# A hybrid decoder block on one core: rotary DMAs and the rotary table moved to the load queue, an eviction put first, keys split a step sooner, two multiplications moved in the tail

## The chip, the core and the metric

The kernel runs on one core of one Trainium2 chip. The core has five engines that run side by side, each with its own instruction queue that it works through in order: PE (TensorE, matmuls), ACT (ScalarE), DVE (VectorE), POOL (GpSimd) and SP (SyncE, which here does nothing but start DMAs). They wait for each other through semaphores. DMAs are started from the queues of SP and ACT; an engine that starts a DMA first waits, like for any other instruction, until what the DMA needs is there, and everything behind it on that engine waits with it. The metric is the device time of one execution in microseconds (us), lower is better. "Span" is the profiled part of one execution, from the first instruction to the last.

## The reference

One layer, everything in float32, 1024 positions of width 1024:

```python
h = x + 1/2 * SwiGLU_1(rms(x))                     # hidden width 2816
u = rms(h);  [q | k | v | p | gate_logits] = u @ W_in
A: q, k: rotate the first 16 of 64 dims (rotary);  12 heads in 3 groups with
   (window, dilation) = (128, 1), (512, 4), (2048, 16); softmax attention;
   the groups are merged per head slot by their softmax denominators; @ W_A
B: p: trailing means over 2/4/8/16 positions minus p, per-group linear map, scale; @ W_B
h = h + (sigmoid(gA) * yA + sigmoid(gB) * yB) @ W_o
h = h + 1/2 * SwiGLU_2(rms(h))
out = rms_final(h)
```

The rotation of a head of q or k, for each position with its angle: `out = [x1*c - x2*s, x2*c + x1*s, rest]`, where x1 and x2 are dims 0 to 7 and 8 to 15 and c, s are a table of cosines and sines over positions.

## The kernel before

**Matrix products.** A float32 operand is split in two parts, a high one (`hi`, a rounded copy made by ACT) and a low one (`lo = x - hi`, by DVE or POOL), and a product is the sum of three matmuls (hi·hi, lo·hi, hi·lo). On top of that the wide products use a seven-product scheme of the Strassen kind: sums and differences of quarter matrices are formed by DVE, seven products are taken instead of eight, and the results are combined. A product of the projections is 12 matmuls of 128x512 (`product`, L316).

**Stages in order of time.** FFN 1 up; FFN 1 down (`Down`, L788: seven products, each in steps of 24 matmuls; ACT L746 makes the high parts `bhi_f` of the weights and `ahi_f` of the activations, L750 the low parts `blo_f`, `alo_f` on DVE or, every fourth, on POOL, L732 loads the activations `g_f`, L766 forms sums of weights); the mixer's projection W_in ("mix"); attention and the pooling branch; W_o; FFN 2 up; FFN 2 down and the final norm ("tail").

**Order of the work.** Most of the kernel stands under `tc.manual_schedule()`: each engine executes in the order in which the Python code issues. So the order of calls in the loops is the order of each engine's queue.

**The table.** In FFN 1 down, a dictionary `tasks` (L1346) hangs small jobs on steps: at step 4 the raw table is loaded in rows by position (`load_rope`), at step 10 `make_tables` (L1312) transposes six 128x128 blocks on PE (L1317), ACT copies them out of PSUM (L1318), and eight DMAs on ACT's queue (L1322) store them in DRAM, ordered for reading back.

**The projection loop** (L1387). `items` lists the products in order, one a step; within an operation the order is (1, 6, 2, 7, 5, 4, 3). In step k: the result of product k-1 is taken out of its bank first if it is a product 1 (`out(1)`); then the operand of step k+2 is formed and split (`mix_operand`: DVE L354, L358, L362, L367 for sums, ACT L304 the high part, DVE or POOL L307 the low part); the sigmoid of a finished gate (`activate`, L1081); the twelve matmuls of product k; the result of product k-1 if it wasn't a 1 (`out`: ACT L1057 for 1, DVE L1060 for 6, ACT L1062 for 2, DVE L1064 for 7, L1068 for 5, L1071 for 4, L1074 for 3); and last the pending jobs in `later`, each a generator that is resumed some steps on. Products 5 and 3 use the same PSUM bank (`key` "v"; 1 and 2 share "x"): product 3 starts from zero in it, so it has to wait until `out(5)` has read it. `raw` tiles are the weights, loaded by SP (L67, L69).

**Jobs.** `rotate` (L1097, six of them, for the pairs of q or k): stores the projected rows to DRAM (L1101, two DMAs), some steps later loads the first 16 dims of each head into one tile `ro` (L1107, two DMAs), shuffles (L1111), multiplies with the table's two parts (L1112, L1113), reloads the table for the next group where it is the last user (`load_table`, L1190, DMA L1195 on SP), adds (L1117), and stores the rotated dims back (L1120, two DMAs). All but the table's load are on ACT's queue. `turn` stores v on SP (L1138). `split_late` splits weights that are needed later and stores them on SP (L1215, L1216, L1220). `window` is the pooling branch (L1151 to L1175).

**Attention** (loop at L1839). A step q takes two blocks of scores (L1592 on PE), exponentials (ACT L1619), transposes the exponentials (PE L1639), splits them (`ehi`, ACT L1651; `elo`, DVE L1654), and multiplies with v (L1672). The q and k of the next group lie in a ring: loaded by SP (L1231), split in quarters by `split_ring` (ACT L1238 the high part, POOL L1239 the low part). For the second group of the ring, `uses[1]`, the quarters are split in steps 3 and 4; they are read by the scores from step 4 on.

**Tail.** In FFN 2 down's last two products DVE adds the result (L793) to h by tiles t; with the product before the last `low_half` (L2150) takes the squares of the low half of tile 4+t (ACT L2153), and for tiles 5 and 6 at once multiplies the low half with the final gain (`with_gain`, DVE L2160); with the last product the high halves follow (L2164), then the norm's power (L2168, L2169) and the scaled output (L2174, L2178, L2184).

## Time and profile before

| | |
|---|---|
| median of 3 runs | 1920.37 us (1918.9 to 1920.75) |
| profiled execution | 1922.71 us |
| its span | 1920.9 us |
| mean granted PE clock | 0.996 |
| mean DMA rate | 172 GB/s |

How to read it: rows of a timeline give the start in us, the duration in us, the engine and line, the operation, `output<-input`, the shape, and in brackets how long the engine stood idle before and what released it. Consecutive similar instructions are one row (xN). A `q` behind an engine's name (SPq, ACTq) is its queue of DMA starts. The granted clock is the share of full TensorE clock that the chip allowed.

### The profile page before, as it was taken

The page shows a single profiled execution, that of the slowest core. Times are in us where ns is not written, and L with a number is a line of the kernel's source. Part 1 is how long each engine was busy: PE and PEld are TensorE (multiplying, and loading weights), DVE is VectorE, ACT ScalarE, POOL GpSimd, SP SyncE. Part 2 cuts the span into 40 slices and gives each one's busy share as a digit, 9 for nine tenths or more (in the row PEclk, how much of TensorE's full clock was granted, in tenths as well). Part 3 has the DMA queues.
Part 4 walks back from the last instruction along what each step waited for, and adds up shares of the span by engine and source line. Part 5 has one row for each costly group of instructions (what it writes and reads, how often), then busy time and mean ns, then how long its engine had stood idle before and what let it go on. Part 6 is the DMA issues. An engine that isn't in the chain of part 4 may idle for free.

```text
span 1920.9 us, 24690 instructions
## 1 busy us (share of the span) xinstructions
PE 1894.7 (99%) x8822; PEld 1566.7 (82%) x8822; DVE 1330.4 (69%) x1975; ACT 772.3 (40%) x1394; POOL 711.1 (37%) x532
## 2 busy tenths in 40 slices
PE   9999999999999998999999999999999999999998
PEld 8888888888778887888887888888888888878886
DVE  6886566557677776667886787888665556577777
ACT  7323333334335542334444673263333333333344
POOL 4433333332122353444555265643333333312131
PEclk9999999999999999999999999999999999999999
DMA  4154223336466636575668877643433223453564
GB/s 188 62 200 155 83 95 125 109 129 209 133 206 218 202 97 183 186 261 188 220 236 307 301 232 266 249 176 119 172 115 127 83 90 120 142 197 132 198 213 164
DMA packets 144131, 330.78 MB, mean 172 GB/s; under 512 B 17672, under 2 KB 39176, under 8 KB 142472
## 3 DMA queue, kind: packets, MB, share of 16 engines
q1 hardware_dynamic: 136008, 308.52, 46.6%
q10 hardware_dynamic: 8000, 20.69, 3.1%
q8 instruction: 69, 1.13, 0.2%
q14 instruction: 54, 0.44, 0.1%
HBM read 229.61 MB, written 99.55 MB: 171 GB/s over the span
## 4 chain that ended last, share of the span: by engine, by line
PE 36%; DVE 4%; DMA 3%; issue 3%; ACT 2%; POOL 2%; SPq 0%; ACTq 0%; DVEq 0%; POOLq 0%
PE d_f L788 7%; PE wo L1984 3%; PE yp L1731 1%; PE u_mixm L316 1%; PE u_f20b L316 1%; PE u_f21a L316 1%; PE u_f210a L316 1%; PE u_f29b L316 1%; PE u_f29a L316 1%; PE u_f28b L316 1%; PE u_f27b L316 1%; PE u_f27a L316 1%; PE u_f26b L316 1%; PE u_f26a L316 1%; PE u_f25b L316 1%
## 5 line engine op out<-in xcount | busy, mean ns | idle before, releaser
L788 PE MATMUL d_f<-bhi_f,alo_f 128*128 128x512 f32 x616 | 241.4, 392 | 3.6 <-POOL alo_f L750 3.0
L788 PE MATMUL d_f<-bhi_f,ahi_f 128*128 128x512 f32 x616 | 241.3, 392 | 1.5 <-ACT ahi_f L746 1.0
L788 PE MATMUL d_f<-blo_f,ahi_f 128*128 128x512 f32 x616 | 240.2, 390 | 0.0
L750 POOL TENSOR_TENSOR alo_f<-g_f,ahi_f 128x512 fp32r<-128x512 f32 x60 | 83.8, 1414 | 281.8 <-ACT ahi_f L746 257.5
L316 PE MATMUL u_mixm<-xhi_t_mix,wc_mixm 128*128 128x512 f32 x608 | 158.8, 392 | 4.1 <-ACT wc_mixm L304 4.1
L788 PEld LDWEIGHTS d_f<-bhi_f,alo_f 128*128 128x128 f32 x616 | 116.0, 188 | 30.9 <-POOL alo_f L750 5.5
L788 PEld LDWEIGHTS d_f<-bhi_f,ahi_f 128*128 128x128 f32 x616 | 116.1, 188 | 26.7 <-ACT ahi_f L746 2.3
L316 PEld LDWEIGHTS u_mixm<-xhi_t_mix,wc_mixm 128*128 128x128 f32 x608 | 114.0, 189 | 28.2 <-ACT wc_mixm L304 4.8
L788 PEld LDWEIGHTS d_f<-blo_f,ahi_f 128*128 128x128 f32 x616 | 116.1, 189 | 23.9
L316 PE MATMUL u_mixm<-xhi_b_mix,wc_mixm 128*128 128x512 f32 x456 | 120.9, 393 | 3.4 <-ACT wc_mixm L304 1.5
L307 POOL TENSOR_TENSOR wc_mixm<-s_mixm,wc_mixm 128x512 fp32r<-128x512 f32 x52 | 78.1, 1503 | 107.9 <-ACT wc_mixm L304 103.6
L316 PEld LDWEIGHTS u_mixm<-xhi_b_mix,wc_mixm 128*128 128x128 f32 x456 | 84.5, 188 | 22.7 <-issue 1.6
L304 ACT ACTIVATE wc_mixm<-s_mixm 128x512 fp32r<-128x512 f32 x76 | 47.5, 628 | 119.6 <-DVE s_mixm L358 44.1
L746 ACT ACTIVATE ahi_f<-g_f 128x1024 fp32r<-128x1024 f32 x84 | 81.9, 975 | 4.4 <-DMA g_f<-gs_f 4.3
L316 PE MATMUL u_mixm<-xlo_t_mix,wc_mixm 128*128 128x512 f32 x304 | 82.0, 392 | 0.0
L307 POOL TENSOR_TENSOR wc_mixm<-raw,wc_mixm 128x512 fp32r<-128x512 f32 x40 | 58.4, 1461 | 48.0 <-ACT wc_mixm L304 36.1
L1984 PE MATMUL wo<-w_o,o_hi 128*128 128x512 f32 x224 | 69.4, 391 | 0.2 <-DVE merge L1799 0.2
L746 ACT ACTIVATE bhi_f<-s_f1w 128x512 fp32r<-128x512 f32 x55 | 32.7, 628 | 89.8 <-DVE s_f1w L766 71.5
L746 ACT ACTIVATE bhi_f<-s_f2w 128x512 fp32r<-128x512 f32 x55 | 32.6, 627 | 89.5 <-DVE s_f2w L766 81.8
L316 PEld LDWEIGHTS u_mixm<-xlo_t_mix,wc_mixm 128*128 128x128 f32 x304 | 57.6, 190 | 12.2
L750 DVE TENSOR_TENSOR alo_f<-g_f,ahi_f 128x1024 fp32r<-128x1024 f32 (+1 forms) x48 | 57.5, 1199 | 8.1 <-ACT ahi_f L746 8.1
L316 PE MATMUL u_mixm<-xlo_b_mix,wc_mixm 128*128 128x512 f32 x228 | 61.1, 390 | 0.0
(1332 smaller groups left out, 4756.3 us busy)
## 6 DMA issues: line engine op xcount, KB each, us to landing
g_f<-gs_f SPq DMA_DIRECT2D x70, 512.0 KB
gs_f<-y_f SPq DMA_DIRECT2D x88, 256.0 KB
raw<-in_w2a_dram SPq DMA_DIRECT2D x35, 512.0 KB
raw<-in_w2b_dram SPq DMA_DIRECT2D x35, 512.0 KB
gs_f<-gb_f SPq DMA_DIRECT2D x46, 256.0 KB
raw<-in_w1a_dram SPq DMA_DIRECT2D x22, 512.0 KB
raw<-in_w3a_dram SPq DMA_DIRECT2D x22, 512.0 KB
raw<-in_w1b_dram SPq DMA_DIRECT2D x22, 512.0 KB
```

The costliest lines, as they stand in the source:

```text
L304: ac.activation(w[:, 0], src, AF.Copy)
L307: eng.tensor_tensor(w[:, 1], src, w[:, 0].bitcast(F32), op=OP.subtract)
L316: pe.matmul(p, a, b, start=(start and n == 0), stop=(n == 11), skip_group_check=not start)
L746: ac.activation(hi[:, c], src, AF.Copy)
L750: eng.tensor_tensor(lo[:, d], src[:, o], hi[:, d].bitcast(F32), op=OP.subtract)
L788: pe.matmul(self.banks[m][t], l, r, start=(first and q == 0), stop=(last and q == 2))
L1731: pe.matmul(p, a, b, start=(j == 0), stop=(j == 11))
L1984: pe.matmul(banks[m][t], l, r, start=(st == 0 and j == 0 and q == 0), stop=(st == 1 and j == 1 and q == 2))
```

## The change

1. The rotation's 36 DMAs (L1101, L1107, L1120) go from ACT's queue to SP's. In `rotate` the table's reload moves one step later, behind the add, and the add moves ahead of the step's end.
2. The table is put in another layout. A copy on POOL (`reorder`, at step 9) interleaves the rows so that the transposes give blocks that one SP DMA stores, in place of the eight on ACT. The two multiplications with the table read it in strips of 128.
3. `out(5)` is treated as `out(1)`: it is issued first in its step, ahead of the next operand's instructions; the sigmoid of a gate then follows a step sooner.
4. `split_ring(uses[1], ...)` is issued in steps 2 and 3 instead of 3 and 4.
5. `with_gain(5)` and `with_gain(6)` are issued with tile 7's low half instead of each with its own tile.

PE's instructions and their order are the same as before. SP goes from 731 instructions to 768, ACT from 1334 to 1290.

```diff
--- before.py
+++ after.py
@@ -1013,7 +1013,7 @@
 
 
     qk_dram = [dram.tile([2, 2, HD, S], F32, name=f"qk{u}") for u in range(HPAIRS * GROUPS)]
-    table_dram = dram.tile([16, 2 * GROUPS, 2, 4, P], F32, name="table")
+    table_dram = dram.tile([2 * GROUPS, P, P], F32, name="table")
     v_dram = [dram.tile([P, 2, S], F32, name=f"v{u}") for u in range(HPAIRS * GROUPS)]
     pool_dram = [dram.tile([P, 2, S], F32, name=f"pool{g}") for g in range(4)]
     gate_dram = [dram.tile([P, 2, S], F32, name=f"gate{d}") for d in range(KT)]
@@ -1098,26 +1098,27 @@
             g, y = self.g, self.y
             u = self.hp * GROUPS + g
             for a in (1, 0):
-                nc.scalar.dma_start(qk_dram[u][a].rearrange("h d c -> (h d) c"), y[a])
+                nc.sync.dma_start(qk_dram[u][a].rearrange("h d c -> (h d) c"), y[a])
                 yield 1
             yield 3
             ro = tmp(f"ro{u}").rearrange("p (a c) -> p a c", a=2)
             places = [qk_dram[u][:, :, :16, c].rearrange("a h r c -> (a h) r c") for c in (LOWS, HIGHS)]
             for t in range(2):
-                nc.scalar.dma_start(ro[t * HD:(t + 1) * HD, 0, :], places[t])
+                nc.sync.dma_start(ro[t * HD:(t + 1) * HD, 0, :], places[t])
             yield 3
             tab = tables[g]
 
             ve.stream_shuffle(ro[:, 1, :], ro[:, 0, :], [i ^ 8 for i in range(32)])
-            ve.tensor_tensor(ro[:, 1, :], ro[:, 1, :], tab[:, 1, :], op=OP.mult)
-            ve.tensor_tensor(ro[:, 0, :], ro[:, 0, :], tab[:, 0, :], op=OP.mult)
+            for n in (1, 0):
+                part = ro[:, n, :].rearrange("p (j c) -> p j c", j=4)
+                ve.tensor_tensor(part, part, tab[:, :, n], op=OP.mult)
+            yield 1
+            ve.tensor_tensor(ro[:, 0, :], ro[:, 0, :], ro[:, 1, :], op=OP.add)
             if self.hp == 1 and g + 1 < GROUPS:
                 load_table(g + 1)
             yield 1
-            ve.tensor_tensor(ro[:, 0, :], ro[:, 0, :], ro[:, 1, :], op=OP.add)
-            yield 1
             for t in range(2):
-                nc.scalar.dma_start(places[t], ro[t * HD:(t + 1) * HD, 0, :])
+                nc.sync.dma_start(places[t], ro[t * HD:(t + 1) * HD, 0, :])
 
         def turn(self):
             yield 1
@@ -1188,10 +1189,10 @@
     tables = {}
 
     def load_table(g):
-        tables[g] = keep.tile([P, 2, HALF], F32, tag="gain", bufs=1, name=f"table{g}_in")
+        tables[g] = keep.tile([P, 4, 2, P], F32, tag="gain", bufs=1, name=f"table{g}_in")
         for t in range(2):
-            src = table_dram[:, 2 * g + t].rearrange("c s j p -> c (s j p)")
-            dst = tables[g][t * HD:(t + 1) * HD].rearrange("p s c -> p (s c)")
+            src = table_dram[2 * g + t].rearrange("(c q) p -> c (q p)", c=16)
+            dst = tables[g][t * HD:(t + 1) * HD].rearrange("p j s c -> p (j s c)")
             nc.sync.dma_start(dst, src[None].to_broadcast([4, 16, 1024]))
 
     def split_late(i):
@@ -1309,17 +1310,19 @@
             given.append(own_row("rope")[:, :768])
             nc.sync.dma_start(given[0].rearrange("p (i c) -> p i c", i=GROUPS * NT), c_rope)
 
+        def reorder():
+            given.append(own_row("turn")[:, :768])
+            src, dst = (v.rearrange("p (b x) -> p b x", b=2 * GROUPS) for v in given)
+            gp.tensor_copy(dst.rearrange("p b (c q) -> p b c q", c=16), src.rearrange("p b (q c) -> p b c q", c=16))
+
         def make_tables(tag):
             tab = own_row("table")[:, :768]
             for c, n in ((0, 4), (4, 2)):
                 p = bank(tag, f"table_{c}")
                 for j in range(n):
-                    pe.transpose(p[:, j * P:(j + 1) * P], given[0][:, (c + j) * P:(c + j + 1) * P], ident)
+                    pe.transpose(p[:, j * P:(j + 1) * P], given[1][:, (c + j) * P:(c + j + 1) * P], ident)
                 ac.activation(tab[:, c * P:(c + n) * P], p[:, :n * P], AF.Copy)
-            tab = tab.rearrange("p (b c) -> p b c", c=P)
-            for n in range(8):
-                j, a = divmod(n, 2)
-                nc.scalar.dma_start(table_dram[:, :, a, j], tab[16 * n:16 * n + 16])
+            nc.sync.dma_start(table_dram.rearrange("b m p -> m b p"), tab.rearrange("p (b c) -> p b c", c=P))
 
         def rows_first(t, tag):
             rs = [Rows(X_mix, "b11", h[t][:, LOWS], t, tag), Rows(X_mix, "b21", h[t][:, HIGHS], t, tag)]
@@ -1345,6 +1348,7 @@
 
         tasks = {
             4: [(load_rope,), (load_small,)],
+            9: [(reorder,)],
             10: [(make_tables, "mm")],
             31: [(inverse, 0)],
             32: [(inverse, 1), (scale_in_place, 0)],
@@ -1385,8 +1389,8 @@
         later, results = [], {}
         load_table(0)
         for k in range(len(items) + 4):
-            if k - 1 in results and items[k - 1][1] == 1:
-                mixes[items[k - 1][0]].out(1, results.pop(k - 1))
+            if k - 1 in results and items[k - 1][1] in (1, 5):
+                mixes[items[k - 1][0]].out(items[k - 1][1], results.pop(k - 1))
             mix_operand(k + 2)
             if k + 3 < len(items) and items[k + 3][1] in (7, 4):
                 mix_operand(k + 3, 2)
@@ -1862,9 +1866,9 @@
             if i > 1 and 0 < u < len(uses) - 1:
                 split_ring(uses[u + 1], i - 2)
                 split_ring(uses[u + 1], i)
-            if q in (3, 4):
-                split_ring(uses[1], q - 3)
-                split_ring(uses[1], q - 1)
+            if q in (2, 3):
+                split_ring(uses[1], q - 2)
+                split_ring(uses[1], q)
             end_branches()
             exponents(2 * q)
             exponents(2 * q + 1)
@@ -2152,8 +2156,9 @@
         y, st = h_tile(f"n4_{t}"), small.tile([P, 4], F32, tag="nlast", name=f"nst_last{t}")
         ac.activation(y[:, LOWS], h[t][:, LOWS], AF.Square, scale=D ** -0.5, accum_out=st[:, 0:1])
         ends[t] = y, st
-        if t in (5, 6):
-            with_gain(t)
+        if t == 7:
+            with_gain(5)
+            with_gain(6)
 
     def with_gain(t):
         y = ends[t][0]
```

## The prediction

> **What bounds the kernel now.** I read the busy shares first, then the list of waits of TensorE (PE), then the timelines of the engines around each wait.
>
> ```profile
> span 1920.9 us, 24690 instructions
> PE 1894.7 (99%) x8822; PEld 1566.7 (82%) x8822; DVE 1330.4 (69%) x1975; ACT 772.3 (40%) x1394; POOL 711.1 (37%) x532
> ```
>
> PE is busy for 1894.7 of 1920.9 us: only 26.2 us are idle. The change leaves PE's instructions and their order alone, so it can win only idle time or time at a low clock. The waits of PE (engine, tile, line, what it waited for: us in total, times, longest) say which idle time is in reach:
>
> ```profile
> PE u_mixm L316 <- ACT wc_mixm L304: 5.7, 3, 4.1
> PE d_f L788 <- POOL alo_f L750: 3.0, 6, 0.7
> PE s L1592 <- POOL xhi_b_mix L1239: 1.3, 1, 1.3
> PE u_mixm L316 <- ACT y_m L1057: 0.7, 2, 0.4
> ```
>
> There is a second loss. Cut into windows (length, five busy times, granted clock, DMA share, GB/s), three stretches of 20 us have a low clock:
>
> ```profile
> 500.00:520.00 20.00, 18.64 (x73) 14.33 (x72) 12.54 (x18) 6.44 (x9) 4.99 (x4) 0.91 0.49 150
> 760.00:780.00 20.00, 16.72 (x67) 13.73 (x68) 11.37 (x16) 5.89 (x11) 7.51 (x6) 0.91 0.86 312
> 1060.00:1080.00 20.00, 18.70 (x130) 16.30 (x129) 13.23 (x44) 13.75 (x44) 5.05 (x4) 0.91 0.85 311
> ```
>
> In each, 20 x (1 - 0.91) = 1.8 us of clock is missing. PE's timeline shows what that is:
>
> ```profile
> 508.83 0.50 PE L788 MATMUL d_f<-bhi_f,alo_f 128*128 128x512 f32 x1 [0.62 <-POOL alo_f L750]
> 509.16 0.39 PE L788 MATMUL d_f<-bhi_f,ahi_f 128*128 128x512 f32 x1
> 509.39 0.39 PE L788 MATMUL d_f<-blo_f,ahi_f 128*128 128x512 f32 x1
> 510.51 0.79 PE L788 MATMUL d_f<-bhi_f,alo_f 128*128 128x512 f32 x1 [0.73 <-POOL alo_f L750]
> 511.09 0.63 PE L788 MATMUL d_f<-bhi_f,ahi_f 128*128 128x512 f32 x1
> 511.52 0.63 PE L788 MATMUL d_f<-blo_f,ahi_f 128*128 128x512 f32 x1
> ```
>
> Matmuls that follow each other 0.23 us apart (509.16, 509.39) are 0.43 us apart (511.09, 511.52) behind stalls of 0.62 and 0.73 us. All three low windows hold a stall sum of 1.3 us or more (1.35 here, 4.15 and 1.30 below). I therefore charge 1.8 us to each of these three stalls, beside the stall itself. That is a reading from three cases. [...] What follows if they only coincide is the second rival.
>
> **Part 1, rotations on the load queue: 6.65 us.** ACT, SP's queue, DVE and PE around 752 us, and the waits of SP there:
>
> ```profile
> SPq L1195 <- DVE ro L1113: 11.3, 1, 11.3
> 748.01 1.03 SPq L67 DMA_DIRECT2D raw<-in_w_qkv_dram  x2
> 752.22 0.46 ACTq L1101 DMA_DIRECT2D qk<-y_m  x1
> 753.22 0.62 ACT L304 ACTIVATE wc_mixm<-s_mixm 128x512 fp32r<-128x512 f32 x1
> 762.23 0.33 ACTq L1101 DMA_DIRECT2D qk<-y_m  x1
> 762.60 0.63 ACT L304 ACTIVATE wc_mixm<-s_mixm 128x512 fp32r<-128x512 f32 x1 [8.76 <-DMA raw<-in_w_qkv_dram]
> 763.28 2.07 PE L316 MATMUL u_mixm<-xhi_t_mix,wc_mixm 128*128 128x512 f32 x4 [4.15 <-ACT wc_mixm L304]
> 768.82 0.67 DVE L354 TENSOR_TENSOR s_mixm<-raw 128x512 f32<-128x512 f32 x1
> ```
>
> ACT ends L304 at 753.84 and stands until 762.23, where a store L1101 goes out; the row names a raw load as what it waited for, and the newest ones went out at 748.01, late, because SP had held 11.3 us in the table load for DVE's L1113. The split L304 that PE needs is queued behind that store, and PE loses 4.15 us. With the store on SP, L304 at 762.60 waits for nothing but DVE and PE, so the 4.15 us and the 1.8 us of clock go. The two waits on ACT's y_m L1057 (0.7 us together) stand behind L1101's issues on ACT as well (the first behind the one at 752.22) and go: 4.15 + 1.8 + 0.7 = 6.65.
>
> All 36 rotation DMAs (12 of L1101, 12 of L1107, 12 of L1120) now queue on SP. New waits there: L1101 on DVE's last two results, L1107 on the landing of the stores, L1120 on DVE's add. Behind them stand raw loads, v stores, table loads and the stores of late weights. The table load itself goes out a step later, behind the raw loads instead of ahead of them, so raw leaves up to 11.3 us earlier there. The spare time: raw of 748.01 had landed by 762.23 (14.2 us at most) and is first read at 768.82 (L354), so 6.6 us are left. A hold below that costs nothing; one of 8.4 us, as ACT had, would be too long. I take 0, because the 11.3 us hold that goes is the longer; both ends are kept (rival four). On DVE the two multiplications of a rotation read strips of 128 elements instead of 512. L354's row, of the same 128x512, has 0.67 us; strided they cost between nothing and as much again, and with DVE busy for 1330.4 of 1920.9 us I take 0 (at the other end 12 x 0.67 = 8 us of DVE, spread over six rotations).
>
> **Part 2, the table in one store: 3.15 us.**
>
> ```profile
> 500.00 5.28 ACTq L1322 DMA_DIRECT2D table<-table  x8
> 505.32 1.15 ACT L746 ACTIVATE bhi_f<-s_f1w 128x512 fp32r<-128x512 f32 x2 [5.35 <-DMA table<-table]
> 507.50 2.95 POOL L750 TENSOR_TENSOR alo_f<-g_f,ahi_f 128x512 fp32r<-128x512 f32 x2 [17.21 <-PE d_f L788]
> 491.96 0.41 SPq L732 DMA_DIRECT2D g_f<-gs_f  x1
> 511.57 1.04 ACT L746 ACTIVATE ahi_f<-g_f 128x1024 fp32r<-128x1024 f32 x1
> ```
>
> Eight issues hold ACT for 5.28 us; then come bhi, ahi, and POOL's alo, for which PE waited 0.62 and 0.73 us. Without the issues ACT's two splits can start 5.3 us sooner, four times what is missing, so 1.35 + 1.8 = 3.15 go. The added POOL copy (128x768) is not in the trace: POOL's pass over 128x512 takes 2.95 / 2 = 1.48 us, so 2.2 us for half as many again, between nothing and twice that; it lies in 17.21 us of idle POOL. Without that cover it would push alo by its length, 2.2 us. The store now waits on SP for ACT's copy of the transposed table, which ended just ahead of the issues (500.00). The load of 491.96 and those behind it go out up to 8 us later, at about 500; the first of them is read by ACT at 511.57 (one step after that of 506), 11.5 us on. I take 0; the price if they are late is in rival one.
>
> **Part 3, fifth result first: 2.4 us.**
>
> ```profile
> 700.31 0.68 DVE L1068 TENSOR_TENSOR y_m<-u_mixm,y_m 128x512 f32<-128x512 f32 x1
> 701.14 1.17 PE L316 MATMUL u_mixm<-xhi_b_mix,wc_mixm 128*128 128x512 f32 x4 [0.96 <-ACT wc_mixm L304]
> 729.15 1.16 PE L316 MATMUL u_mixm<-xhi_b_mix,wc_mixm 128*128 128x512 f32 x4 [0.55 <-ACT wc_mixm L304]
> 949.42 0.94 PE L316 MATMUL u_mixm<-xhi_b_mix,wc_mixm 128*128 128x512 f32 x3 [0.27 <-DVE y_m L1068]
> 1008.42 0.68 DVE L307 TENSOR_TENSOR wc_mixm<-raw,wc_mixm 128x512 fp32r<-128x512 f32 x1
> 1009.84 1.15 PE L316 MATMUL u_mixm<-xhi_b_mix,wc_mixm 128*128 128x512 f32 x4 [0.99 <-DVE y_m L1068]
> ```
>
> The list blames ACT for the first two, but PE starts 0.15 us after L1068 ends (700.99, 701.14), as at 949.42: product 3 reuses the bank that L1068 reads. Now L1068 goes ahead of the next operands. That frees 0.96 + 0.55 + 0.27. At 1009 only L307 is passed, which moves L1068 0.6 us forward (1008.42 to 1009.02): 0.6 of 0.99. Sum 2.4, at most 2.77. The operands behind it start 0.6 us later; PE has a product of some 2.7 us in between, so I price that at 0 (at most 0.6 x 4 = 2.4, which would undo the part).
>
> **Part 4, keys split a step sooner: 2.5 us.**
>
> ```profile
> 1050.03 11.47 DMA xhi_b_mix<-qk
> 1061.08 0.51 ACT L1619 ACTIVATE e<-e,stats 128x256 f32<-128x256 f32 x1
> 1064.27 1.09 PE L1639 MATMUL tp<-ident,e 128*128 128x128 f32 x8
> 1069.27 0.33 PE L1592 MATMUL s<-xhi_b_mix,xlo_b_mix 64*128 64x128 f32 x2 [1.30 <-POOL xhi_b_mix L1239]
> ```
>
> PE waited 1.30 us for POOL's low half of the new keys, and 1.8 us of clock followed. The splits (ACT L1238, POOL L1239) now stand ahead of the four exponentials that begin at 1061.08. But the first half of the keys lands at 1061.50 (1050.03 + 11.47, from the chain of waits), and the second was issued behind it. So a new wait: ACT stands there. With the second landing 1.3 us on (an estimate: 0.5 MB at the 311 GB/s of the third window row is 1.7 us, and nothing if both moved side by side; I take a value near the former) and a split of 0.6 us on each (as L304's 0.62), the exponentials begin at 1063.4 and end at 1065.4 (4 x 0.5). The transposes that read them ran at 1064.27, the second half of the eight from 1064.8: I charge a new stall of 0.6 us, between 0 and 1.3 + 1.8 (then nothing is won). 1.3 + 1.8 - 0.6 = 2.5.
>
> **Part 5, tail: 0.5 us.**
>
> ```profile
> 1903.65 0.69 DVE L2160 TENSOR_TENSOR n<-h_last,gain_final 128x512 f32<-128x512 f32 x1 [0.19 <-ACT n L2153]
> 1906.26 0.50 PE L788 MATMUL d_f<-bhi_f,ahi_f 128*128 128x512 f32 x1 [0.80 <-ACT ahi_f L746]
> ```
>
> Two multiplications of 0.69 us (L2160 for tiles 5 and 6) leave DVE's chain ahead of the last weight split, where PE waited 0.80 us, and stand later, ahead of the last sums. The stall goes, but the 1.4 us come back on DVE behind PE's last products. Between 0 and 0.9; I take 0.5.
>
> **Sum:** 6.65 + 3.15 + 2.4 + 2.5 + 0.5 = 15.2. The profiled execution took 1922.71 us (span 1920.9 and 1.8 around it), so it would be 1907.5; the median of the three runs, 1920.37, is 2.3 lower: 1905.2.
>
> **Rivals.**
> 1. Loads behind the table store are late, and the key split only moves its stall: parts 2 and 4 give nothing. 1905.2 + 3.15 + 2.5 = 1910.9. For it: SP's hold of 8 us, the landing at 1061.50. Against: 11.5 us from issue to use, and only half a microsecond of overhang in part 4.
> 2. The low clock has another cause and stays in all three places: 1905.2 + 5.4 = 1910.6. For it: only three cases. Against: the half rate begins within a matmul of the stall. [...]
> 3. The rotation's move doesn't do what it says: ACT's 8.76 us were a wait for raw itself, which comes as late as before. Then 4.15 + 1.8 stay, and with rival one's losses too: 1910.9 + 5.95 = 1916.8, no change that can be told. Against: raw is first read by DVE at 768.82, over six us later.
> 4. Slower: SP, in order, now holds where ACT held. A hold of 8.4 us ahead of a raw load with 6.6 us to spare makes PE late by 1.8 us and costs 1.8 us of clock, 3.6 a rotation. At six rotations 21.6: 1905.2 + 21.6 = 1926.8. It decides from 6.6 us of hold, in five of six rotations (15.2 / 3.6 = 4.2). For it: DMA share 0.86 there, landings of 11 to 14 us. Against: the 11.3 us hold that goes.
>
> **How the numbers follow.** Forecast 0.50, rival one 0.18, two 0.12, three 0.09, four 0.11. The prediction is the forecast, 1905.2. Low end: the larger bounds of parts 3 to 5 (0.4 + 0.6 + 0.4) and 0.9, half the spread of the runs of before (1918.9 to 1920.75), give 1902.9; I write 1902.5. The high end reaches past rivals one and two to just short of three: 1916; that is 0.80. What this kernel's measurement can tell from no change is about 0.2%, 3.8 us: faster (below 1916.6) 0.80, same 0.09, slower 0.11.
>
> **What would show it.** Right: no wait on L304 over 1 us near 763; no eight-fold issue on ACT near 500 and no wait on alo_f at 508; the waits on L1068 down to one of some 0.4 us; a clock of 1.00 in the three windows. Wrong: SP waits on L1101 or L1107 over 6.6 us with a PE wait on s_mixm or wc_mixm behind them (rival four); a PE wait on L1639 near 1065 with the low clock still there (one); low windows without a stall ahead of them (two).

## The result, and the profile after

The changed kernel takes 1908.91 us (median of 4 runs, 1905.97 to 1910.77) against 1920.56 us (4 runs, 1918.9 to 1921.24): a ratio of 0.9939, with a 95% interval of 0.9922 to 0.9956. That is 11.65 us less, where 15.2 were forecast. The profiled executions are 13.8 us apart (1922.71 and 1908.91 us), because the profiled run of before lies 2.2 us above its median.

The page of the changed kernel, and the waits of PE (us in total, times, longest):

```profile
span 1907.0 us, 24693 instructions
PE 1888.8 (99%) x8822; PEld 1564.4 (82%) x8822; DVE 1328.2 (70%) x1975; ACT 774.4 (41%) x1394; POOL 713.7 (37%) x533
```
```profile
PE tp L1643 <- ACT e L1623: 2.4, 1, 2.4
PE d_f L788 <- POOL alo_f L750: 1.4, 3, 0.7
...
PE u_mixm L316 <- DVE y_m L1068: 0.5, 1, 0.5
...
PE u_mixm L316 <- ACT wc_mixm L304: 0.2, 1, 0.2
```

PE's busy time fell too, from 1894.7 to 1888.8 us, with the same 8822 instructions: two low stretches are gone, each of 3.41 us at half the clock in the trace, so about 1.7 us lost in each, 3.4 of the 5.9. The 5.7 us on ACT's L304 are 0.2, L1068 has one wait left, the list has no wait on L1239/L1240 (the keys' low halves) any more. At its head stands a wait that wasn't there: 2.4 us for the exponentials. The windows (granted clock third from the end):

```profile
500.00:520.00 20.00, 20.00 (x90) 16.55 (x89) 14.34 (x21) 8.02 (x12) 5.08 (x4) 1.00 0.63 194
760.00:780.00 20.00, 20.00 (x90) 16.53 (x90) 10.96 (x17) 6.91 (x14) 9.75 (x8) 1.00 0.67 229
1050.00:1070.00 20.00, 17.52 (x131) 14.81 (x130) 11.90 (x44) 13.20 (x43) 5.09 (x4) 0.91 0.71 253
```

Two of the three low stretches are gone, PE is busy all 20 us in both windows; the third moved along with its stretch. Between the first microseconds and the tail the clock's record in the trace has no other.

PE executes the same list in both kernels, so the start of one and the same matmul can be compared, and each step of the difference has a place:

| PE's instruction | before | after | PE ahead by | step, and the part it belongs to |
|---|---|---|---|---|
| first of the kernel's own | 6.29 | 6.01 | 0.28 | chance at the start |
| d_f, end of the table's stretch | 513.65 | 509.82 | 3.83 | +3.55, part 2 |
| u_mixm, ahead of the long wait | 750.10 | 744.50 | 5.60 | +1.8, part 3 at 701 and 729, small waits |
| u_mixm, behind it | 766.43 | 754.38 | 12.05 | +6.45, part 1 |
| u_mixm at part 3's last place | 1009.84 | 996.05 | 13.79 | +1.7, part 1 at 819 (0.6), part 3 at 949 and 1009 |
| yp, behind the keys' stretch | 1073.71 | 1061.20 | 12.52 | -1.27, part 4 |
| last of all | 1913.33 | 1899.13 | 14.20 | +1.7: 1.2 at the last weight split, part 5; 0.4 at 1718, no part |
| the span | 1920.9 | 1907.0 | 13.9 | -0.3, DVE's tail behind PE, part 5 |

Parts 1, 2, 3 and 5 gave what was forecast or a little more. Part 4 was to give 2.5 us and took 1.3. This is its place in the changed kernel: ACT's timeline, PE's, and the piece of the chain of waits that holds the load of the second half of the keys, with the store that SP waited for ahead of it (start, us, what):

```profile
1046.35 1.09 ACT L1655 ACTIVATE ehi<-tp 128x512 fp32r<-128x512 f32 x2 [0.77 <-PE tp L1643]
1050.55 0.63 ACT L1239 ACTIVATE xlo_b_mix<-xhi_b_mix 128x512 fp32r<-128x512 f32 x1 [3.10 <-DMA xhi_b_mix<-qk]
1051.82 0.63 ACT L1239 ACTIVATE xlo_b_mix<-xhi_b_mix 128x512 fp32r<-128x512 f32 x1 [0.64 <-DMA xhi_b_mix<-qk]
1052.35 0.49 ACT L1623 ACTIVATE e<-e,stats 128x256 f32<-128x256 f32 x1
```
```profile
1052.99 2.17 PE L1643 MATMUL tp<-ident,e 128*128 128x128 f32 x8 [2.42 <-ACT e L1623]
```
```profile
1026.56 13.16 DMA late_w<-raw
1039.79 12.00 DMA xhi_b_mix<-qk
```

ACT stands at the splits from 1047.4 to 1050.55 and again to 1051.82, as the forecast said, 1.3 us apart, as it estimated. But in before the first half landed at 1061.50, here at 1050.5: 11.0 us earlier, while PE and ACT were 13.8 us earlier. The keys came 2.8 us later for those that wait for them. The DMA engines in that stretch (length, busy times, clock, DMA share, GB/s), in the changed kernel and in before:

```profile
1040.00:1050.00 10.00, 10.00 (x75) 8.12 (x75) 6.65 (x23) 6.52 (x22) 0.00 (x0) 1.00 1.02 389
1050.00:1060.00 10.00, 7.52 (x55) 6.01 (x53) 5.02 (x21) 7.46 (x23) 5.09 (x4) 0.83 1.02 374
```
```profile
1050.00:1060.00 10.00, 9.86 (x70) 7.45 (x70) 5.80 (x25) 7.07 (x22) 0.00 (x0) 1.00 1.02 395
```

The share is 1.02 in both, against 0.63 to 0.71 in the windows of 20 us above: the DMA engines are full. That such a stretch doesn't move forward as far as the compute ahead of it is the explanation to be tested.

### The profile page after: what moved, and what is told of

Same layout as the page of the kernel before. It is cut to its first block, busy times and chain, and to the rows that moved or that the text cites. A ratio compares the mean times of both kernels' runs of the same rounds, so it can differ in the third digit from the quotient of the medians.

```text
span 1907.0 us, 24693 instructions
## 1 busy us (share of the span) xinstructions
PE 1888.8 (99%) x8822; PEld 1564.4 (82%) x8822; DVE 1328.2 (70%) x1975; ACT 774.4 (41%) x1394; POOL 713.7 (37%) x533
## 5 line engine op out<-in xcount | busy, mean ns | idle before, releaser
L750 POOL TENSOR_TENSOR alo_f<-g_f,ahi_f 128x512 fp32r<-128x512 f32 x60 | 83.4, 1407 | 276.0 <-ACT ahi_f L746 276.0
L304 ACT ACTIVATE wc_mixm<-s_mixm 128x512 fp32r<-128x512 f32 x76 | 47.1, 629 | 110.4 <-DVE s_mixm L358 53.6
L750 DVE TENSOR_TENSOR alo_f<-g_f,ahi_f 128x1024 fp32r<-128x1024 f32 (+1 forms) x48 | 57.6, 1200 | 7.4 <-ACT ahi_f L746 7.4
```

The lines of the kernel that those rows point to most:

```text
L304: ac.activation(w[:, 0], src, AF.Copy)
L750: eng.tensor_tensor(lo[:, d], src[:, o], hi[:, d].bitcast(F32), op=OP.subtract)
```

## The experiments

The theory: part 4's wait is set by the landing of the keys in that full stretch, and is small where PE isn't ahead of it. The rivals: splits ahead of the exponentials cost 2 us or more wherever the kernel stands; or part 4 gains as forecast and the 2.4 us have another source. For part 1 the question was which of its two halves, the queue or the table's later reload, took the long wait away.

All results in one table: the median, that of the kernel before measured beside it, their ratio with its 95% interval, and how far PE's last instruction lies from that of the changed kernel in the profiled execution. An interval reaches some 2 to 3 us to either side, so finer differences between two variants are read from the traces.

| kernel | us | before | ratio (interval) | PE's last instruction |
|---|---|---|---|---|
| the changed kernel | 1908.91 | 1920.56 | 0.9939 (0.9922 to 0.9956) | at 1899.13 |
| part 4 undone | 1906.41 | 1920.61 | 0.9924 (0.9909 to 0.9938) | 3.4 sooner |
| before with part 4 alone | 1921.14 | 1920.61 | 0.9996 (0.9987 to 1.0005) | 11.5 later |
| keys loaded first | 1906.14 | 1919.20 | 0.9934 (0.9920 to 0.9947) | 4.0 sooner |
| table stored on ACT | 1905.45 | 1920.08 | 0.9921 (0.9906 to 0.9936) | 4.8 sooner |
| part 3 undone | 1909.69 | 1920.08 | 0.9943 (0.9928 to 0.9958) | 0.8 later |
| rotations on ACT | 1912.12 | 1920.08 | 0.9959 (0.9947 to 0.9971) | 0.3 later |
| table reloaded early | 1912.85 | 1920.08 | 0.9960 (0.9946 to 0.9974) | 4.4 later |
| part 1 undone | 1913.56 | 1919.20 | 0.9967 (0.9957 to 0.9976) | 5.3 later |
| part 5 undone | 1909.09 | 1920.61 | 0.9935 (0.9918 to 0.9952) | 1.8 later |
| one low half on DVE | 1905.58 | 1920.61 | 0.9919 (0.9904 to 0.9934) | 3.6 sooner |
| both low halves on DVE | 1905.76 | 1919.20 | 0.9931 (0.9919 to 0.9944) | 4.3 sooner |
| both halves on DVE, table on ACT | 1903.55 | 1919.20 | 0.9920 (0.9906 to 0.9933) | 5.6 sooner |

**Part 4 undone in the changed kernel.**

```diff
-            if q in (2, 3):
-                split_ring(uses[1], q - 2)
-                split_ring(uses[1], q)
+            if q in (3, 4):
+                split_ring(uses[1], q - 3)
+                split_ring(uses[1], q - 1)
```

> The changed kernel with part 4 alone undone: the next keys are split in steps 3 and 4 again. Theory (the keys are late by the memory): in the changed kernel PE runs 13.8 us ahead of the kernel before when attention begins, but the two halves of the keys land only about 11.0 us ahead (1050.5 and 1051.8 us), since the DMA engines are full there; ACT, which has the splits ahead of the exponentials, stands until then, and PE waits 2.4 us for the exponentials. With the splits back behind them the wait on the transposes (2.4 us) goes, POOL's 1.3 us and the low clock (1.8 us) stay: about 1.2 us less than the changed kernel, 1907.7 us. Rival (the forecast's price was right, and the 2.4 us come from elsewhere): part 4 is worth 2.5 us, so undoing it gives 1911.4 us.

Measured: 1906.41 us, 2.5 us less than the changed kernel. The intervals of the two ratios overlap, so it is the trace that tells: PE ends 3.4 us sooner, 0.6 of which it was ahead before it came to the keys. PE's timeline and a window of this run:

```profile
1054.94 0.33 PE L1596 MATMUL s<-xhi_b_mix,xlo_b_mix 64*128 64x128 f32 x2 [1.30 <-POOL xhi_b_mix L1240]
```
```profile
1045.00:1065.00 20.00, 18.70 (x145) 16.35 (x141) 13.81 (x48) 13.74 (x45) 5.05 (x4) 1.00 0.92 340
```

The wait on the transposes is gone and POOL's 1.30 us are back, as the theory said; the rival's 1911.4 falls. But the clock stays at 1.00 behind the same 1.30 us that had a low stretch behind them in before. So undoing gains more than the 1.2 us expected.

**Part 4 alone in the kernel before** (the same lines the other way round).

> The kernel before with part 4 alone. Theory: here PE is not ahead, so the keys land at 1061.5 and 1062.8 us with PE's transposes at 1064.3 us; PE waits about 0.6 us on the exponentials, the 1.3 us on POOL and the low clock behind it go: 2.5 us less than before, 1918.0 us. Rival (the place of the splits costs 2.4 us wherever the kernel stands, because ACT takes them in order): a wait of 2 us or more on the transposes, the low clock stays, 1921 us or more.

Measured: 1921.14 us (10 runs, 1917.14 to 1922.12): no change by the times. That is the rival's number; its signs, a long wait on the transposes and a low clock, aren't in the trace. ACT and PE in it:

```profile
1062.20 0.63 ACT L1238 ACTIVATE xlo_b_mix<-xhi_b_mix 128x512 fp32r<-128x512 f32 x1 [0.46 <-DMA xhi_b_mix<-qk]
1063.47 0.63 ACT L1238 ACTIVATE xlo_b_mix<-xhi_b_mix 128x512 fp32r<-128x512 f32 x1 [0.64 <-DMA xhi_b_mix<-qk]
```
```profile
1064.81 1.27 PE L1639 MATMUL tp<-ident,e 128*128 128x128 f32 x6
```

ACT waits 0.46 us where the changed kernel waited 3.10, PE has no listed wait on the transposes (it loses some 0.7 us over the eight of them), and over the stretch from 1060 to 1074 PE gains 2.4 us on before, 1.7 of them the low stretch that this run doesn't have there. So in this trace the forecast's 2.5 us came out. In its time they don't show, because PE loses 1.8 us again at 819, in a wait of 2.23 us on ACT's y_m L1057, where before had 0.39: ACT stood 4.42 us at a rotation store, 2.59 in before. That the other nine runs lose the gain the same way is not shown; the interval (2.5 us less to 1.0 more) just leaves room for it.

**Keys loaded ahead of the branch weights**, in the changed kernel:

```diff
-        load_branch(1)
         load_ring(uses[1], ring_place(1))
+        load_branch(1)
```

> The changed kernel with the loads of the next keys issued ahead of the 0.5 MB load of the branch weights instead of behind it; part 4 as it is. Theory (PE's 2.4 us come from the landing of the keys, in a stretch where the DMA engines are full): 0.5 MB less ahead of them at some 390 GB/s brings both halves 1.3 us sooner, and PE waits 1.1 us instead of 2.4; with luck no low clock: 1.3 to 3 us less, 1906 to 1907.6 us. Rival (the wait is set by ACT's order, or SP is held as long in front of the keys by the DMAs issued eight places before): the same wait within 0.5 us, 1908.9 us; the branch weights late would show as a wait of PE on their products.

Measured: 1906.14 us, 4.0 us sooner at PE's end in the trace; by the ratios only 1 us, which can't be told. The chain of this run:

```profile
1035.72 12.51 DMA xhi_b_mix<-qk
```

The second half goes out at 1035.72 us instead of 1039.79 and lands at 1048.23 (1035.72 + 12.51) instead of 1051.79, 3.6 us sooner where 1.3 were expected, and the wait on the transposes is gone altogether. The order on ACT is that of the changed kernel: the landing sets the wait, and the theory stands. That all 3.6 us come from the order is not shown: the landing varies from run to run, as the next run has it.

**The table's store on ACT's queue** (one DMA, in the changed kernel):

```diff
-            nc.sync.dma_start(table_dram.rearrange("b m p -> m b p"), ...)
+            nc.scalar.dma_start(table_dram.rearrange("b m p -> m b p"), ...)
```

> The changed kernel with the table's single store on ACT's queue instead of SP's. Theory one (the eight issues were the cost, 5.28 us of ACT): one issue takes some 0.5 us of ACT, PE has no wait on the low halves near 508 us, SP is not held from 492 to 500 us, and the loads behind are 8 us earlier, which PE doesn't notice: as the changed kernel within 1 us. Theory two (any DMA issue on ACT there is too late for PE, or the hold on SP costs something that the trace shows as DVE waiting on weights at 506.5 us, 0.02 us after they landed): a difference of 1 us or more either way.

Measured: 1905.45 us, 3.5 us less: theory two by the size, though not for either of its reasons alone. The issue costs ACT 0.39 us, and SP isn't held:

```profile
499.95 0.39 ACTq L1325 DMA_DIRECT2D table<-table  x1
500.38 1.15 ACT L746 ACTIVATE bhi_f<-s_f1w 128x512 fp32r<-128x512 f32 x2 [0.46 <-ACT table L1324]
```

In the changed kernel SP held its loads until 500.26, after its store at 499.80:

```profile
499.80 0.37 SPq L1325 DMA_DIRECT2D table<-table  x1
500.26 0.49 SPq L732 DMA_DIRECT2D g_f<-gs_f  x1
500.81 0.73 SPq L69 DMA_DIRECT2D raw<-in_w2a_dram  x1
```

PE didn't wait for those loads at once, as forecast; but by 570 us it is 1.8 us ahead of the changed kernel, since three waits of 0.20, 0.53 and 0.41 us from 562 to 570 us are absent. They are absent in the last experiment too, which also stores the table on ACT; in the changed kernel and its nine variants with the store on SP they come to between 0.28 and 1.14 us. So they go with the store's place; that it is the hold on SP by which it makes them is argued, not shown. The rest is the wait on the transposes, 0.75 us here with the full clock behind it: in this run the second half of the keys landed at 1048.06, 3.7 us sooner than in the changed kernel, with PE only 2.1 us ahead of it there. It also went out 4.3 us sooner:

```profile
1035.50 12.56 DMA xhi_b_mix<-qk
```

**Part 3 undone:**

```diff
-            if k - 1 in results and items[k - 1][1] in (1, 5):
-                mixes[items[k - 1][0]].out(items[k - 1][1], results.pop(k - 1))
+            if k - 1 in results and items[k - 1][1] == 1:
+                mixes[items[k - 1][0]].out(1, results.pop(k - 1))
```

> The changed kernel with part 3 alone undone: the fifth result is taken out of its bank behind the next operand again. Theory: PE's four waits come back at the third product (0.96, 0.55, 0.27, and 0.99 where 0.49 is left): 2.3 to 3.0 us more, 1911.2 to 1911.9 us. Rival (the operands that part 3 delays had eaten some of the gain, or the four waits shrink because SP's loads come earlier): 1 us or less more.

Measured: 1909.69 us, 0.8 us more, not told from the changed kernel by the times. The rival's number, but not for its reason: the four waits are back (0.95, 0.55, 0.27, 1.03 us), PE is 2.3 us behind at 998 us, and then it waits less for the keys and stays at the full clock:

```profile
PE tp L1643 <- ACT e L1623: 2.0, 1, 2.0
```

Of the 2.3 us, 0.4 are a wait that is shorter at the keys, and about 1.0 is the low stretch that the changed kernel has behind that wait and this run hasn't, behind almost the same wait. So what is gained ahead of the keys' landing is waited away at it only in small part; most of the rest is chance of the clock.

**Part 1's two halves.** Rotations back on ACT, the later reload kept; and the reload back ahead of the add, rotations kept on SP:

```diff
-  nc.sync.dma_start(...)      # L1101, L1107, L1121
+  nc.scalar.dma_start(...)
```

> The changed kernel with the 36 rotation DMAs back on ACT's queue; the later reload of the table stays. Theory one (the queue decides, as the forecast had it): ACT stands at a rotation store again until an older DMA has landed, the split behind it is late, PE waits 3 to 4 us for it near 753 us and may run at the low clock behind it: 3 to 6 us more than the changed kernel, 1912 to 1915 us. Theory two (the table's reload decides): the weights went out at 748.0 us in the kernel before because SP stood 11.3 us in front of them, and went out at 737.1 us in the changed kernel; with the reload behind the add they are early on any queue, so the DMA that ACT's store has to wait for has landed by about 747 us: no wait over 1 us on ACT's split there, 1909 us.

Measured: 1912.12 us (1909.56 to 1915.91), 3.2 us more. The profiled execution is the fastest of them and lies between the two theories. The long wait isn't back, but a wait for ACT's eviction is, 1.48 us behind a rotation's issue, and three on L1068 (1.7 us together, where the changed kernel has one of 0.5):

```profile
748.75 1.20 PE L316 MATMUL u_mixm<-xhi_b_mix,wc_mixm 128*128 128x512 f32 x4 [1.48 <-ACT y_m L1057]
```

```diff
-            yield 1
             ve.tensor_tensor(ro[:, 0, :], ro[:, 0, :], ro[:, 1, :], op=OP.add)
-            if self.hp == 1 and g + 1 < GROUPS:
-                load_table(g + 1)
-            yield 1
+            (the reload, then a yield, stand ahead of the add; a yield behind it)
```

> The changed kernel with the table's reload put back one step sooner, ahead of the add; the rotation DMAs stay on SP. Theory one (the queue decides): SP stands 9 to 11 us in front of the weights again, which go out near 738 to 740 us of this kernel's clock plus that hold, but nothing on ACT is behind it, and they are first read 20 us later: no wait of PE over 1 us near 753 us, 1909 us. Theory two (the table's reload decides): the weights are late and PE waits 2 us or more on them or on their sums, 1911 to 1914 us.

Measured: 1912.85 us, 3.9 us more. The number is theory two's, but both theories named the wrong place. SP, DVE and PE in this run:

```profile
767.55 1.15 SPq L1107 DMA_DIRECT2D ro<-qk  x2
```
```profile
774.00 0.01 DVE L1111 LOAD_MASK_SELECT ro<-ro  x1 [8.62 <-DMA ro<-qk]
```
```profile
780.84 0.90 PE L316 MATMUL u_mixm<-xhi_b_mix,wc_mixm 128*128 128x512 f32 x2 [3.79 <-DVE y_m L1068]
```

It is not the weights that are late for PE but the rotation's own load, which SP issues behind its holds (at 762.57 us in the changed kernel; the rotation's store, whose landing it waits for, goes out at 759.05 instead of 753.87). DVE, in order, stands 8.62 us at the shuffle; L1068, which PE needs, is queued behind it, and PE waits 3.79 us. This is the forecast's fourth rival (SP holds where ACT held) with the damage on another path: it happens at one rotation, when the reload is early.

**Part 1 wholly undone:**

> The changed kernel with part 1 wholly undone: the rotation DMAs on ACT's queue and the table's reload ahead of the add. Theory (the two halves of part 1 stand in for each other only in part): with both undone SP holds the weights for DVE, ACT's store waits for them to land, and PE waits some 4 us for ACT's split near 752 us, beside the 0.3 and 0.4 us on ACT's evictions: 5 to 6.7 us more than the changed kernel, 1914 to 1915.6 us, less what PE then waits less for the keys (up to 2.4 us). Rival (each half costs by itself what its own run showed, 2.7 us of PE for the queue and 5.2 us for the reload, and they add): 7.9 us more, 1916.8 us.

Measured: 1913.56 us, 4.65 us more, or 5.4 by the ratios. The wait of before is back:

```profile
757.51 0.63 ACT L304 ACTIVATE wc_mixm<-s_mixm 128x512 fp32r<-128x512 f32 x1 [8.31 <-DMA raw<-in_w_qkv_dram]
```
```profile
758.19 1.22 PE L316 MATMUL u_mixm<-xhi_t_mix,wc_mixm 128*128 128x512 f32 x2 [3.71 <-ACT wc_mixm L304]
```

PE is 8.2 us behind the changed kernel at 764 us, 3.4 of them low clock. That is the rival's sum (2.7 and 5.2), though the waits are others; 1.9 us come back at the keys and 1.0 more because the low stretch there is absent, so that the time is the theory's. Either half of part 1 alone takes the long wait on ACT's split away; the queue alone back on ACT leaves 1.48 us at an eviction, the early reload alone 3.79 us at another place. The later reload is what keeps the weights, and the rotation's load, from being late.

**Part 5 undone** (`with_gain(t)` for tiles 5 and 6 at once):

> The changed kernel with part 5 alone undone. By the traces PE gained 1.4 us at the last weight split, and the last PE instruction was 14.2 us sooner while the span was only 13.9 us shorter: undoing part 5 brings PE's wait of 0.8 us back and costs 1.1 us, 1910.0 us. Rival (the forecast): 0.5 us, 1909.4 us. A difference of less than about 1.5 us is told by the traces, not by the times.

Measured: 1909.09 us, 0.2 us more: the times can't tell. PE ends 1.8 us later in the trace, of which 0.7 were there ahead of the tail; its wait at the last split is 0.39 us, not the 0.80 expected. In the changed kernel the moved pair stands on DVE in the tail:

```profile
1893.02 1.29 DVE L2165 TENSOR_TENSOR n<-h_last,gain_final 128x512 f32<-128x512 f32 x2
```

**What the runs together say of the keys.** In the changed kernel and the ten variants of it with the order of loads as it is, the second half lands later against PE than in before, by 0.9 to 2.8 us: 2.8 in the changed kernel (PE ahead by 13.8), 1.1 with the table stored on ACT (15.8), 2.4 with part 3 undone (11.5), 0.9 with part 1 undone (5.5). So the lag is there in each of them, but it doesn't grow in step with the lead.

The traces show more of its cause than the share of 1.02 does. The landing of each half stands in them as sixteen updates of a semaphore, and in the changed kernel ACT's two splits start 0.03 us behind the last one (1050.55 behind 1050.52, 1051.82 behind 1051.79). There fifteen updates of the second half are in by 1049.29 us and the last comes at 1051.79, 2.50 us behind; in before, and with the table on ACT, it comes 0.91 and 0.96 us behind. The last part of the store `late_w`, for which SP waits before it issues the second half, is late in the same way: 2.00 us behind in the changed kernel, 0.15 with the table on ACT. The second half went out behind it, at 1039.79 and 1035.50, and from there it took 12.00 and 12.56 us. Over the runs the lag goes with this gap of the last part (2.2 us with part 3 undone, 1.1 with part 1 undone). Why the last of the sixteen falls behind, no run shows; that the landing sets PE's wait is shown (2.42 us, and none with the keys loaded first, where the second half landed 3.6 us sooner).

**A better place for the keys' split.** Steps 3 and 4 as in before, with step 3's second low half on DVE, or both (`split_ring` takes the engine as an argument here, POOL if none is given):

```diff
+            if q in (3, 4):
+                split_ring(uses[1], q - 3)                          # both: ve if q == 3
+                split_ring(uses[1], q - 1, ve if q == 3 else gp)
```

> The changed kernel with part 4 replaced: the keys are split in steps 3 and 4 as before, but the second low half of step 3 is made by DVE instead of POOL, so that the two low halves are made side by side. Theory: POOL needs 1.27 us for each half, so the second comes about 1.3 us sooner; PE's wait on the scores (1.3 us) goes and with it the low clock (1.8 us): 4.3 us less than the changed kernel, 1904.6 us. Rival (DVE, which is on the path of the next values, is late by its 0.7 us and PE waits there): a wait of 0.7 us or more on DVE, 1906 to 1908 us.

> As the kernel with one of step 3's two low halves on DVE, but both on DVE. There POOL's half and DVE's half ran side by side, DVE's took 1.37 us instead of 0.69, and PE still waited 0.63 us. Theory (the two slow each other down): one behind the other on DVE they take 0.7 us each and end 0.6 us sooner; no wait on the scores; 0.6 us less than that kernel, 1905.0 us. Rival (DVE needs 1.3 us for each for another reason, such as the strides of the operands): the second ends 1.2 us later and PE waits 1.8 us, 1907 us.

Measured: 1905.58 and 1905.76 us. PE's wait on the scores is 0.63 us with one half on DVE and 0.31 with both. The halves, side by side on DVE and POOL (first run), and one behind the other on DVE (second run):

```profile
1053.44 1.37 DVE L1240 TENSOR_TENSOR xhi_b_mix<-xhi_b_mix,xlo_b_mix 128x512 fp32r<-128x512 f32 x1 [0.15 <-ACT xlo_b_mix L1239]
```
```profile
1052.96 1.29 POOL L1240 TENSOR_TENSOR xhi_b_mix<-xhi_b_mix,xlo_b_mix 128x512 fp32r<-128x512 f32 x1 [20.48 <-ACT xlo_b_mix L1239]
```
```profile
1053.00 1.28 DVE L1240 TENSOR_TENSOR xhi_b_mix<-xhi_b_mix,xlo_b_mix 128x512 fp32r<-128x512 f32 x2
```

Two on DVE took 1.28 us; the one with POOL at work beside it took 1.37. Each theory holds in part: the halves come sooner, but waits of 0.63 and 0.31 us are left where none was forecast, and the low stretch that the first run was to save is absent with part 4 undone as well. Between the two the times show no difference, and against part 4 undone (1906.41) hardly one.

**Both that gained, together** (both halves on DVE, the table's store on ACT):

> Both changes that gained: step 3's low halves both on DVE with the keys split in steps 3 and 4, and the table's one store on ACT's queue. Theory (they are independent; the table's store on ACT gained 1.8 us of PE before 570 us, the split's place 3.6 us at the end): 1903.0 to 1903.8 us, and no PE wait over 0.6 us between 450 and 1100 us. Rival (the gain before 570 us was chance from run to run, as PE's waits near 563 us vary): as with the low halves alone, 1905 us.

Measured: 1903.55 us (1902.56 to 1903.94), 5.4 us less than the changed kernel, 3.6 by the ratios; its span, 1901.4 us, is the shortest. The time and the condition are the theory's. The largest waits of PE behind the kernel's first 25 us are 0.7 us (L750) and 0.5 (L1068); the one on the keys' low halves is 0.3. It has the lowest time of all, but its ratio can't be told from those of the table stored on ACT or of the one half on DVE, so the times don't show that the two gains add; nor does PE's end (5.6 us sooner, against 4.8 and 4.3).

## Why the prediction was right, and where it was not

The time lies in the range (1902.5 to 1916) and on the forecast side; four of the five terms were sized near enough, one had the wrong sign. That 13.9 us came out in the profiled runs where 15.2 were forecast is in part luck: part 4 fell 3.8 us short, and 0.7 us of what made up for it belong to no part (0.28 at the start, 0.4 at 1718).

- **What bounds the kernel:** PE's idle time and its clock, as said. PE's busy time fell by 5.9 us and its idle time by 8.0 (26.2 to 18.2), together the 13.9 of the span.
- **Part 1, forecast 6.65:** 6.45 at the long wait (low clock included) and 0.6 at 819. With the part undone ACT's hold of 8.31 us came back, so the wait was what the forecast said. But it gave the whole term to the queue, and the later reload alone, with the rotations on ACT, takes the long wait away too. That the new waits on SP cost nothing was right only because the reload moved: with the reload early they cost 3.79 us.
- **Part 2, forecast 3.15:** 3.55. The store's price on SP, taken as 0, was 0 at the stretch itself; with a single store on ACT (0.39 us of issue) PE has no wait there either, so the eight issues (5.28 us) were the cost, not ACT's queue. No run undoes the part as a whole; its size is PE's lead at 513 us, before any other part acts.
- **Part 3, forecast 2.4:** 2.3 by undoing it, with 0.49 us left at 996 us, where 0.4 was forecast. At the end of the kernel without it only 0.8 is seen, mostly because that run lacks a low stretch.
- **Part 4, forecast +2.5, measured -1.3:** the step that failed is "the first half of the keys lands at 1061.50 (1050.03 + 11.47)", with the transposes "at 1064.27". Both were read from one trace, and the four other parts move the second by 13.8 us and the first by 11.0. With part 4 alone in the kernel before the step holds (2.4 us gained in the trace, none by the times). The stall was taken as 0.6, between 0 and 3.1; it was 2.42, and the low clock stayed.
- **Part 5, forecast 0.5:** some 1 us at PE's end, less 0.3 behind it; not resolved by the times.
- **The low clock:** charged at 1.8 us behind each stall of 1.3 us or more. That is too firm: 0.62 and 0.70 us at the same place in the kernel before with part 4 alone had none behind them (below), nor had 1.30 us with part 4 undone. The profiled run of before happened to have all three, and a mean clock of 0.996; of 37 other runs of before only 4 have 0.996, and 32 have 0.997 or 0.998. One low stretch is worth some 0.0009 of it (1.7 of 1920 us), so most runs had fewer to lose. That is probably much of why the profiled difference is 13.8 us and that of the medians 11.65.
- **The rivals:** the first was half right (the key split moved its stall). The second was too: the low clock went with its stall in two of the three places, but not because a stall of that length always brings it. The third and fourth didn't occur, but the fourth's mechanism appeared in an experiment.

## What to carry to other kernels

A landing time read from a trace holds for that trace: when the change speeds up what comes ahead, compute moves forward and a stretch in which the DMA engines are full may move less (here, at a share of 1.02, by 0.9 to 2.8 us), so check every wait on a transfer there against the new, earlier need, and look at what its issue waited for as well as at its landing. An instruction that waits for a transfer goes behind the ones that don't (the keys' splits ahead of the exponentials cost PE 2.42 us); and moving a queue's DMAs elsewhere moves its holds along, so look for what stands behind them there too (with the reload early, DVE stood 8.62 us for a load that SP had issued late, and PE 3.79). To value parts, compare the start of the same matmul in both traces; the end of the kernel alone hides what a later wait swallows, or what chance of the clock adds.

## What the runs showed of the hardware

**The low clock behind a stall is not a matter of its length alone.** The kernel before with part 4 alone, with stalls of 0.62 and 0.70 us at 508.63 and 510.31, where before had 0.62 and 0.73 and a clock of 0.91, and with a stall of 2.23 us at 819.55; and the changed kernel without part 3 and without part 5, with waits of 1.98 and 2.00 us on the transposes:

```profile
500.00:520.00 20.00, 18.67 (x81) 14.51 (x80) 12.66 (x18) 6.44 (x9) 5.19 (x4) 1.00 0.49 146
810.00:830.00 20.00, 17.77 (x79) 14.37 (x78) 11.76 (x15) 5.63 (x11) 7.88 (x6) 1.00 0.81 285
```
```profile
1045.00:1065.00 20.00, 17.85 (x135) 14.72 (x133) 13.91 (x45) 13.98 (x44) 5.07 (x4) 1.00 0.95 363
```
```profile
1045.00:1065.00 20.00, 17.95 (x128) 14.82 (x128) 12.74 (x40) 12.98 (x42) 5.07 (x4) 0.91 0.92 348
```

The waits of 1.98 and 2.00 us stand at the same place, and only the second has a low stretch behind it; so it is with the 1.30 us on the keys' low halves, which had one in before and none with part 4 undone. In the clock's record of before the three low stretches begin at 510.55, 763.13 and 1070.33 us, each 3.41 us long at half the clock; they begin 252.59 and 307.20 us apart, 74 and 90 times 3.413. The one of the changed kernel, at 1053.33, is 3.41 us long too. PE's waits there are 1.35 us in two, 4.15, 1.30 and 2.42 us. Length alone doesn't decide: the 1.48 us with the rotations on ACT, longer than the 1.30 of before, had no low stretch behind them (four matmuls took 1.20 us there, with a mean clock of 0.999 over the run; four behind the 4.15 us of before took 2.07). What decides stays open.

**One subtraction on DVE beside one on POOL.** The low half of 128x512 took DVE 1.37 us where POOL had begun the other one 0.48 us before (1053.44 and 1052.96, one half on DVE), and 0.64 us each, 1.28 for two, with POOL idle (both halves on DVE). POOL's took 1.29 us beside DVE's, and two took 2.52 us with DVE at other instructions (part 4 undone). It is one case; why DVE's took longer there, and whether the one that starts first is never slowed, no run shows.

**The last of a load's sixteen updates came up to 2.50 us behind the fifteenth.** In a stretch with a DMA share of 1.02 it was 0.91 us for the second half of the keys in before, 0.96 with the table's store on ACT and 2.50 in the changed kernel.
